# A sample's state update is issued behind the weight split written in front of it

## The chip, the core and the metric

The kernel runs on one core of a Trainium2 chip. The metric is the device time of one execution in microseconds; three runs of the kernel before took between 1820.84 and 1825.6 us, with a median of 1822.57 us. The engines are named as in the profile: PE (TensorE) multiplies matrices, DVE (VectorE) and ACT (ScalarE) work element by element, POOL (GpSimd) and SP (SyncE) here mostly issue DMA transfers. Each engine takes its own instructions strictly one after the other: an instruction that waits holds up everything behind it on the same engine.

## What is computed

One layer of a decoder runs for 256 positions of a prompt and for one new position of each of 8 samples, 264 columns in all. A wide projection feeds three branches: a spatial gate (A), an HGRN2 recurrence (B) and a gated linear attention, GLA (C). The branches are projected, gated, summed and projected again; then comes an MLP with 8192 hidden channels. For the samples the two recurrences are a single step on a stored state:

```
S_new = f[:, None] * S_old + k[:, None] * v[None, :]     # one head: 128 x 128 (HGRN2) or 128 x 256 (GLA)
o     = S_new.T @ q
```

There are 8 HGRN2 heads and 4 GLA heads for each of 8 samples. Each S_new is an output, and o goes on into the layer.

## The kernel before

**The weights.** All weights stream from memory through one long list of items, each a block of four 128-row slices by 256 columns (two slices by 512 columns at one place). SP loads an item into raw tiles (`raw`, line 623; four buffers). Products are made at full precision by splitting every weight in two: ACT casts one half of an item, 128x512, to `whi` (line 631), and DVE subtracts it from the raw value to give `wlo` (line 633, through the helper at line 113). There are six buffers each of `whi` and `wlo`, that is, three items of two halves. PE multiplies an item with three products for each tile (lines 671 to 673: `whi` by the high part of the activations, `whi` by their low part, `wlo` by the high part). One item so multiplied is a "granule" below: 24 products, 12 for each half.

At the end of a granule `ahead()` writes the split of the items up to three ahead of the one just multiplied. After granule number n, therefore, 2(n + 3) halves have been written. The split of the last of them needs the buffers that granule n has just given back.

**The work beside it.** After each granule `background()` (line 725) runs. It raises a counter `now` and takes steps from generators: `bg` with the prompt's recurrences (`mixer_r`) and `bs` with the samples' state updates (`samples_r`, line 1105). There are three groups, two of HGRN2 with four heads and one step per sample, and the GLA group with two steps per sample (two heads each): 32 steps in all.

A step n of `samples_r` writes, in this order: POOL's fetch of the state of step n+2 (`st`, line 1120; four buffers), POOL's broadcast load of the values of step n+1 from a scratch in memory (`vbc`, line 1126; two buffers), a pause until the state of step n was fetched three granules ago and its values two granules ago (`FETCHED`, line 1143), ACT's scaling of the state by f (line 1146, one instruction per head), DVE's multiply-add of k and v (line 1148, one per head), and POOL's store of the result (line 1149). When a sample is complete it is queued for `slot()` (line 692), where PE multiplies the state with q (line 712) at least two granules later; a fetch into a buffer waits for that product to have read it.

**Who orders what.** In this part of the kernel the written order is binding for PE and POOL alone (`manual_schedule`, line 1011). For DVE, ACT and SP the framework's scheduler chooses the order of the queue when the program is built, from its own estimates of when each instruction will be ready. Semaphores guard the data whichever order it chooses.

Of the kernel before, what the change touches and what calls it, by code (L numbers as in the profile page):

```python
# [7 lines left out]
F32 = mybir.dt.float32  # L8
F32R = mybir.dt.float32r
I32 = mybir.dt.int32  # L10
AF = mybir.ActivationFunctionType
ALU = mybir.AluOpType
# [6 lines left out]
NP = 256  # L19
# [45 lines left out]
def hybrid_step_kernel(  # L65
# [9 lines left out]
    V, S, T = nc.vector, nc.scalar, nc.tensor  # L75
# [13 lines left out]
    def nm(s):  # L89
        uid[0] += 1  # L90
        return f"{s}_{uid[0]}"

    def blk(shape=None, dt=F32):
        shape = shape or [P, 4, NT]
        return blkp.tile(shape, dt, tag="b", name=nm("b"))
# [4 lines left out]
    def tmp(shape, tag, bufs=2):  # L100
        return tp.tile(shape, F32, tag=tag, name=nm(tag), bufs=bufs)
# [4 lines left out]
    def mul(o, a, b):  # L106
        V.tensor_tensor(o, a, b, op=ALU.mult)  # L107
# [4 lines left out]
    def sub(o, a, b):  # L112
        V.tensor_tensor(o, a, b, op=ALU.subtract)  # L113
# [100 lines left out]
    def rstd_small(ms, scale, out):  # L214

        n, w = out.shape
        xx, aa = tmp([P, 16], "sx")[0:n, 0:w], tmp([P, 16], "sa")[0:n, 0:w]
        c = 0
        for m in ms if isinstance(ms, list) else [ms]:
            V.tensor_scalar(xx[:, c:c + m.shape[1]], m, scale, EPS, ALU.mult, ALU.add)  # L220
            c += m.shape[1]
        V.tensor_scalar(out.bitcast(I32), xx.bitcast(I32), -0.5, 1597463007.0, ALU.mult, ALU.add)
        for _ in range(3):
            mul(aa, out, out)
            V.scalar_tensor_tensor(aa, aa, -0.5, xx, ALU.mult, ALU.mult)
            V.scalar_tensor_tensor(out, aa, 1.5, out, ALU.add, ALU.mult)
# [370 lines left out]
    class Stream:  # L597
# [28 lines left out]
        def half_hi(self, i):  # L626
            n, width = self.items[i][2], self.items[i][4]
            hi = splp.tile([P, n // 2, width], F32R, tag="whi", name=nm("whi"))
            lo = splp.tile([P, n // 2, width], F32R, tag="wlo", name=nm("wlo"))
            raw = self.raw[i].pop(0)  # L630
            S.copy(hi, raw)  # L631
            self.parts.setdefault(i, []).append((hi, lo))
            return lambda: sub(lo, raw, hi.bitcast(F32))

        def split_half(self, i):
            self.half_hi(i)()
# [22 lines left out]
    stream = []  # L659
# [445 lines left out]
    def samples_r(G):  # L1105

        dv = G.dv
        nj, nh = dv // P, 512 // dv
        q, k, g = G.q, G.k, G.g
        fs = tmp([P, 4, NS], "fs")  # L1110
        S.activation(fs, g[:, :, NP:NT], AF.Exp)
        qm = blk([P, 4, NS, 32])
        mul(qm, q[:, :, NP:NT].unsqueeze(3).to_broadcast([P, 4, NS, 32]),
            delta.rearrange("p (b c) -> p b c", b=NS).unsqueeze(1).to_broadcast([P, 4, NS, 32]))
        steps = [(b, h) for b in range(NS) for h in range(0, 4, nh)]
        ahead, vals = [], []

        def fetch(b, h):
            st = tmp([P, nh, dv], "st", ST_BUFS)
            nc.gpsimd.dma_start(st, G.s_in(b, h, nh))  # L1120
            ahead.append((st, now[0]))

        def values(b, h):
            v = tmp([P, 4, P], "vbc", VB_BUFS)
            r0 = 4 * nj * b + h * nj
            nc.gpsimd.dma_start(v, vs_d[G.i, r0:r0 + 4, :].partition_broadcast(P))
            vals.append((v.rearrange("p (h j) v -> p h (j v)", h=nh), now[0]))

        for s in steps[0:2]:
            fetch(*s)  # L1130
            yield
        values(*steps[0])
        yield
        os_ = tmp([P, dv], f"os{G.i}", 1)
        sts = []
        for n, (b, h0) in enumerate(steps):
            if n + 2 < len(steps):

                yield lambda: len(sts) + sum(len(x[3]) for x in samples) <= ST_BUFS - 3
                fetch(*steps[n + 2])  # L1140
            if n + 1 < len(steps):
                values(*steps[n + 1])
            yield lambda: now[0] >= max(ahead[0][1] + FETCHED, vals[0][1] + FETCHED - 1)
            st, v = ahead.pop(0)[0], vals.pop(0)[0]
            for i in range(nh):
                S.activation(st[:, i, :], st[:, i, :], AF.Copy, scale=fs[:, h0 + i, b:b + 1])  # L1146
            for i in range(nh):
                V.scalar_tensor_tensor(st[:, i, :], v[:, i, :], k[:, h0 + i, NP + b:NP + b + 1], st[:, i, :], ALU.mult, ALU.add)  # L1148
            nc.gpsimd.dma_start(G.s_out(b, h0, nh), st)  # L1149
            sts.append(st)  # L1150
            if h0 + nh == 4:
                samples.append((now[0], (G, qm, os_), b, sts))
                sts = []
            yield
        yield lambda: not samples
        yield READY
        ss, rr = tmp([P, 1], "sss", 1), tmp([P, 1], "srr", 1)
        S.activation(tmp([P, dv], "vt"), os_, AF.Square, accum_out=ss)
        rstd_small(ss, 1.0 / dv, rr)
        S.activation(os_, os_, AF.Copy, scale=rr)  # L1160
        G.os = os_
        yield

    def mixer_r(G):
# [18 lines left out]
        q, k, g = G.q, G.k, G.g  # L1183

        bs.g.append(samples_r(G))


# [660 lines left out]
```

## Time and profile before

One execution was profiled. It is the source of every line shown in the prediction.

| | |
|---|---|
| median of 3 runs | 1822.57 us |
| the profiled execution's own time | 1821.44 us |
| its span, first to last instruction | 1819.4 us |
| mean granted TensorE clock | 0.998 |
| DVE busy | 1179.1 us (65%) |
| ACT busy | 997.2 us (55%) |
| state scaling on ACT, line 1146 | 96 instructions, 37.2 us, first at 369.4 us, last at 791.1 us |
| state update on DVE, line 1148 | 96 instructions, 34.2 us, first at 382.4 us, last at 797.5 us |

In the lines of the profile `out<-in` names the tile written and those read, `L1148` is a line of the kernel, and "x96" counts instructions. "idle before" is the time that an engine sat without work just before the instructions of a group, with what ended it. A row of the waits reads: engine and line that waited, what it waited for, then total us, times, longest us. In a timeline the columns are start, duration (both us), engine, line, operation, tiles, count, and in brackets the idle time before with its releaser. A row that merges "x2" gives the time from the first's start to the last's end.

### The profile page before, as it was taken

The page shows a single profiled execution, that of the slowest core. Times are in us where ns is not written, and L with a number is a line of the kernel's source. Part 1 is how long each engine was busy: PE and PEld are TensorE (multiplying, and loading weights), DVE is VectorE, ACT ScalarE, POOL GpSimd, SP SyncE. Part 2 cuts the span into 40 slices and gives each one's busy share as a digit, 9 for nine tenths or more (in the row PEclk, how much of TensorE's full clock was granted, in tenths as well). Part 3 has the DMA queues.
Part 4 walks back from the last instruction along what each step waited for, and adds up shares of the span by engine and source line. Part 5 has one row for each costly group of instructions (what it writes and reads, how often), then busy time and mean ns, then how long its engine had stood idle before and what let it go on. Part 6 is the DMA issues. An engine that isn't in the chain of part 4 may idle for free.

```text
span 1819.4 us, 42092 instructions
## 1 busy us (share of the span) xinstructions
PE 1780.7 (98%) x16970; PEld 1690.5 (93%) x16970; DVE 1179.1 (65%) x2077; ACT 997.2 (55%) x1824; POOL 138.3 (8%) x228
## 2 busy tenths in 40 slices
PE   7999999999999999999999999999999999999998
PEld 5889999989989988989999989999999999999998
DVE  5566668787576686566555667555666666666666
ACT  5344454666756756655445666454554545454544
POOL 4222000111111111210000000000000000000000
PEclk9999999999999999999999999999999999999999
DMA  9997587788788788897978954877666666666663
GB/s 325 379 347 282 196 293 247 218 260 295 230 285 262 228 261 302 274 326 241 305 252 267 330 166 153 251 255 222 196 195 193 196 196 195 198 196 194 195 193 118
DMA packets 330179, 442.05 MB, mean 243 GB/s; under 512 B 14946, under 2 KB 276944, under 8 KB 329984
## 3 DMA queue, kind: packets, MB, share of 16 engines
q1 hardware_dynamic: 311872, 380.52, 64.7%
q0 software_dynamic: 17184, 57.85, 8.9%
q8 instruction: 133, 2.18, 0.5%
q10 hardware_dynamic: 928, 0.99, 0.2%
q14 instruction: 62, 0.51, 0.1%
HBM read 427.60 MB, written 11.70 MB: 241 GB/s over the span
## 4 chain that ended last, share of the span: by engine, by line
PE 83%; issue 3%; DVE 3%; DMA 3%; ACT 1%; POOL 0%; ACTq 0%; DVEq 0%; SPq 0%; POOLq 0%
PE mm L671 25%; PE mm L673 25%; PE mm L672 25%; PE ada L383 3%; DMA vbc<-vs_d 2%; DVE wlo L113 1%; PE ada L315 1%; PE sm L893 1%; DMA raw<-in_w_in_dram 1%; DVE b L113 1%; PE sm L712 0%; ACT whi L631 0%; PE sm L705 0%; DMA araw<-in_w_ada_dram 0%; PE sm L1617 0%
## 5 line engine op out<-in xcount | busy, mean ns | idle before, releaser
L671 PE MATMUL mm<-b,whi 128*128 128x264 f32 x4600 | 1284.5, 279 | 7.5 <-ACT b L116 3.9
L673 PE MATMUL mm<-b,wlo 128*128 128x264 f32 x4600 | 1272.5, 277 | 6.4 <-DVE wlo L113 4.9
L672 PE MATMUL mm<-b,whi 128*128 128x264 f32 x4600 | 1271.3, 276 | 0.7 <-DVE b L113 0.7
L113 DVE TENSOR_TENSOR wlo<-raw,whi 128x512 fp32r<-128x512 f32 x1136 | 768.8, 689 | 430.4 <-ACT whi L631 427.0
L631 ACT CAST whi<-raw 128x512 fp32r<-128x512 f32 x1136 | 689.0, 616 | 628.9 <-DVE wlo L113 318.9
L671 PEld LDWEIGHTS mm<-b,whi 128*128 128x128 f32 x4600 | 870.8, 189 | 48.2 <-issue 24.8
L673 PEld LDWEIGHTS mm<-b,wlo 128*128 128x128 f32 x4600 | 870.8, 189 | 8.6 <-DVE wlo L113 7.0
L672 PEld LDWEIGHTS mm<-b,whi 128*128 128x128 f32 x4600 | 871.1, 189 | 1.3 <-DVE b L113 1.1
L110 DVE TENSOR_TENSOR b<-b,mm 128x528 f32<-128x528 f32 (+1 forms) x137 | 95.6, 699 | 73.4 <-PE mm L673 65.8
L1148 DVE SCALAR_TENSOR_TENSOR st<-vbc,b,st 128x128 f32<-128x128 f32 (+1 forms) x96 | 34.2, 391 | 54.8 <-DMA vbc<-vs_d 49.9
L1146 ACT ACTIVATE st<-st,fs 128x128 f32<-128x128 f32 (+1 forms) x96 | 37.2, 431 | 51.7 <-DMA st<-in_state_hgrn_dram 29.5
L1785 POOL TENSOR_TENSOR gs<-b,G 128x16 f32<-128x16 f32 x1 | 0.2, 222 | 714.1 <-DVE b L110 714.1
L502 POOL DMA_DIRECT2D b<-in_w_ada_dram x64 | 46.3, 726 | 38.4 <-PE ada L315 31.6
L383 PE MATMUL ada<-araw,cT 128*32 128x512 f32 x296 | 40.8, 601 | 0.4 <-DMA araw<-in_w_ada_dram 0.4
L315 PE MATMUL ada<-b,cT 128*32 128x256 f32 (+1 forms) x640 | 35.2, 358 | 2.1 <-DMA b<-in_w_ada_dram 1.9
L107 DVE TENSOR_TENSOR b<-b,b 128x512 f32<-128x512 f32 (+1 forms) x47 | 34.0, 743 | 1.3 <-ACT b L1260 1.1
L1149 POOL DMA_DIRECT2D out_dram<-st x32 | 23.5, 736 | 132.0 <-DVE st L1148 132.0
L315 PEld LDWEIGHTS ada<-b,cT 128*32 128x32 f32 x640 | 18.2, 114 | 14.2 <-DMA b<-in_w_ada_dram 5.6
L383 PE MATMUL ada<-b,cT 128*32 128x512 f32 x216 | 26.2, 593 | 0.0
L113 DVE TENSOR_TENSOR b<-gt,b 128x528 fp32r<-128x528 f32 x32 | 22.8, 712 | 3.2
L113 DVE TENSOR_TENSOR b<-b 128x1024 f32<-128x1024 f32 (+1 forms) x24 | 24.4, 1019 | 0.0
L1671 ACT ACTIVATE b<-vt 128x528 fp32r<-128x528 f32 x32 | 22.9, 714 | 1.0
(366 smaller groups left out, 902.4 us busy)
## 6 DMA issues: line engine op xcount, KB each, us to landing
raw<-in_w_in_dram SPq DMA_DIRECT2D x231, 512.0 KB, 5.0
raw<-in_w_mlp_up_dram SPq DMA_DIRECT2D x128, 512.0 KB, 3.9
raw<-in_w_mlp_down_dram SPq DMA_DIRECT2D x128, 512.0 KB, 3.6
araw<-in_w_ada_dram SPq DMA_DIRECT2D x74, 512.0 KB, 5.7
b<-in_w_ada_dram SPq DMA_DIRECT2D x54, 512.0 KB, 6.4
b<-in_w_ada_dram POOLq DMA_DIRECT2D x48, 512.0 KB, 10.4
raw<-in_w_branch_dram SPq DMA_DIRECT2D x48, 512.0 KB, 4.5
raw<-in_w_out_dram SPq DMA_DIRECT2D x32, 512.0 KB, 4.9
```

The lines of the kernel that those rows point to most:

```text
L107: V.tensor_tensor(o, a, b, op=ALU.mult)
L110: V.tensor_tensor(o, a, b, op=ALU.add)
L113: V.tensor_tensor(o, a, b, op=ALU.subtract)
L315: T.matmul(acc[32 * j:32 * j + 32, 0:n], cT[:, k, :], w[:, n * j:n * j + n], start=k == 0, stop=k == KT - 1)
L383: T.matmul(self.acc[32 * j:32 * j + 32, :], cT[:, k, :], ws[j // 2][:, j % 2 * 512:j % 2 * 512 + 512], start=k == 0, stop=k == KT - 1)
L502: queue.dma_start(w[:, i], w1[k * P:(k + 1) * P, :, self.k0 * P:(self.k0 + self.n) * P])
L631: S.copy(hi, raw)
L671: T.matmul(o, a, xh(k + j), start=first and j == 0, stop=False)
L672: T.matmul(o, a, xl(k + j), start=False, stop=False)
L673: T.matmul(o, b, xh(k + j), start=False, stop=last and j == n - 1)
L1146: S.activation(st[:, i, :], st[:, i, :], AF.Copy, scale=fs[:, h0 + i, b:b + 1])
L1148: V.scalar_tensor_tensor(st[:, i, :], v[:, i, :], k[:, h0 + i, NP + b:NP + b + 1], st[:, i, :], ALU.mult, ALU.add)
```

## The change

`half_hi` keeps the last cast and the last subtraction that have been written. `samples_r` wraps the scaling and the update of each step in `issue_after`, which adds an edge from each ACT instruction in the block to that last cast and from each DVE instruction in it to that last subtraction. The edge is one of issue order on the same engine: it adds no semaphore. Nothing else changes: the same instructions, tiles, buffers and transfers, and the written order of PE and POOL is what it was.

```diff
@@ half_hi
-            S.copy(hi, raw)
+            self.last = [S.copy(hi, raw).ins, None]
             self.parts.setdefault(i, []).append((hi, lo))
-            return lambda: sub(lo, raw, hi.bitcast(F32))
+
+            def low():
+                self.last[1] = V.tensor_tensor(lo, raw, hi.bitcast(F32), op=ALU.subtract).ins
+
+            return low
@@ samples_r
-            for i in range(nh):
-                S.activation(st[:, i, :], st[:, i, :], AF.Copy, scale=fs[:, h0 + i, b:b + 1])
-            for i in range(nh):
-                V.scalar_tensor_tensor(st[:, i, :], v[:, i, :], k[:, h0 + i, NP + b:NP + b + 1], st[:, i, :], ALU.mult, ALU.add)
+            with tc.issue_after(stream[0].last[0]), tc.issue_after(stream[0].last[1]):
+                for i in range(nh):
+                    S.activation(st[:, i, :], st[:, i, :], AF.Copy, scale=fs[:, h0 + i, b:b + 1])
+                for i in range(nh):
+                    V.scalar_tensor_tensor(st[:, i, :], v[:, i, :], k[:, h0 + i, NP + b:NP + b + 1], st[:, i, :], ALU.mult, ALU.add)
```

## The prediction, made before the changed kernel was seen

> **What bounds the kernel now.** I read the page first, for who is busy.
>
> ```profile
> PE 1780.7 (98%) x16970; PEld 1690.5 (93%) x16970; DVE 1179.1 (65%) x2077; ACT 997.2 (55%) x1824; POOL 138.3 (8%) x228
> ```
>
> PE is busy 98% of the span. A change of order on ACT and DVE can only give back time in which PE stands still, or runs slow, while the state updates are going on. So the second view is the list of PE's waits from 340 to 820 us, the stretch of the state updates.
>
> ```profile
> PE mm L673 <- DVE wlo L113: 4.9, 6, 2.0
> PE sm L705 <- issue: 3.0, 2, 2.3
> PE mm L671 <- ACT whi L631: 1.3, 1, 1.3
> PE mm L673 <- issue: 1.1, 1, 1.1
> PE mm L671 <- ACT gt L1379: 1.0, 1, 1.0
> ```
>
> That is 11.3 us in 11 gaps, and this is the whole stake. Six times PE waits for a subtraction, once for a cast, once for ACT's gate. Three gaps ("issue") have no cause that the profile shows. The third view is the same list for all engines: why are DVE and ACT late?
>
> ```profile
> POOL st L1120 <- PE sm L712: 143.7, 11, 31.3
> POOL out_dram L1149 <- DVE st L1148: 132.0, 17, 28.2
> ...
> DVE st L1148 <- DMA vbc<-vs_d: 49.9, 18, 7.6
> ...
> ACT st L1146 <- DMA st<-in_state_hgrn_dram: 29.5, 9, 8.8
> ACT st L1146 <- DMA st<-in_state_gla_dram: 14.8, 8, 3.0
> ```
>
> DVE stands for 49.9 us in 18 waits with a state update at the head of its queue whose values have not landed; ACT stands for 44.3 us with a scaling whose state has not landed. Subtractions and casts that could run are queued behind them. One such place in detail: first the counts up to 772.89 us, then the timelines of POOL, DVE and PE.
>
> ```profile
> L673 PE MATMUL mm<-b,wlo 128*128 128x264 f32 x1731 | 480.4, 278 | 3.4 <-DVE wlo L113 1.9 <-issue 1.1
> L113 DVE TENSOR_TENSOR wlo<-raw,whi 128x512 fp32r<-128x512 f32 x416 | 274.8, 686 | 83.1 <-ACT whi L631 79.9 <-PE mm L672 1.9 <-PE sm L712 0.7
> ...
> L113 DVE TENSOR_TENSOR wlo<-araw,whi 128x512 fp32r<-128x512 f32 x20 | 12.9, 684 | 0.0
> ```
> ```profile
> 765.56 0.57 POOL L1126 DMA_DIRECT2D vbc<-vs_d  x1
> ```
> ```profile
> 772.90 0.88 DVE L1148 SCALAR_TENSOR_TENSOR st<-vbc,b,st 128x256 f32<-128x256 f32 x2 [7.61 <-DMA vbc<-vs_d]
> 773.70 1.29 DVE L113 TENSOR_TENSOR wlo<-raw,whi 128x512 fp32r<-128x512 f32 x2
> ...
> 777.76 3.70 DVE L113 TENSOR_TENSOR wlo<-raw,whi 128x512 fp32r<-128x512 f32 x6
> ```
> ```profile
> 778.50 0.38 PE L673 MATMUL mm<-b,wlo 128*128 128x264 f32 x1 [1.01 <-DVE wlo L113]
> ```
> ```profile
> 781.17 0.64 PE L712 MATMUL sm<-st,b 128*32 128x256 f32 x8
> ```
>
> PE has run 1731 of these products, four for each half, so it is 432.75 halves into the weights. DVE has subtracted 416 + 20 = 436, only 3.25 halves more, and has stood 7.61 us for values that POOL asked for at 765.56. This update (sample 5, second pair of heads) is written after granule 218, as I count it by following the loops' counters; by then 2 x (218 + 3) = 442 halves are written. The scheduler has put it six halves ahead of its written place. For the 32 steps I count 3 to 23 halves.
>
> **The change part by part.** It removes and adds no instruction. It moves 96 scalings and 96 updates back behind the cast or subtraction written last. On their own engine the moved ones cost the same (37.2 and 34.2 us in all), so what changes is who waits behind them.
>
> *What the waits become.* In its written place the update above follows half 442, whose buffer comes free when PE has done 436. At 772.89 PE still has 3.25 halves to go. A half is 12 products; their pitch stands in PE's timeline at the first stall:
>
> ```profile
> 394.32 0.28 PE L672 MATMUL mm<-b,whi 128*128 128x264 f32 x1
> 394.44 0.28 PE L673 MATMUL mm<-b,wlo 128*128 128x264 f32 x1
> 396.04 0.38 PE L671 MATMUL mm<-b,whi 128*128 128x264 f32 x1 [1.32 <-ACT whi L631]
> 396.25 0.28 PE L672 MATMUL mm<-b,whi 128*128 128x264 f32 x1
> ```
>
> The pitch is 0.11 us, a half 1.3 us, a granule 2.7 us. So the update would come 3.25 x 1.3 = 4.3 us later at the earliest, when the values have long landed. In general, values are asked for at least two granules (5.4 us) ahead of the update's place and are followed by about 1.3 us of cast and subtraction: 6.7 us.
>
> ```profile
> DMA to landing us min/median/max: 3.7/6.6/9.3
> ```
>
> Half of the loads land inside that, the slowest are 2.6 us late. DVE then waits with all splits up to three items ahead done, 8.1 us of PE work. So I cost the remaining wait of DVE at nothing, covered by those items; without that cover it would cost up to 2.6 us a step. The states, fetched three granules (8.1 us) ahead, likewise.
>
> *What comes back on PE.* I assign to the state steps the waits for `wlo` except one (382.49, below), the wait for `whi` and the one for the gate: 4.9 - 0.6 + 1.3 + 1.0 = 6.6 us in seven gaps. A gap costs more than its idle time. From 394.44 to 396.04 are 1.60 us where 0.11 is usual, the next step takes 0.21, so 1.59 us are lost where 1.32 is shown: 0.27 more each, 7 x 0.27 = 1.9 us. And the clock:
>
> ```profile
> 380.00:400.00 20.00, 17.76 (x256) 16.14 (x256) 14.40 (x31) 9.15 (x19) 2.79 (x4) 0.94 0.76 244
> 400.00:420.00 20.00, 20.00 (x361) 18.65 (x361) 17.53 (x33) 13.86 (x26) 4.06 (x7) 0.97 0.91 306
> ...
> 760.00:780.00 20.00, 18.99 (x171) 17.02 (x170) 9.79 (x19) 11.04 (x23) 3.98 (x6) 1.00 0.93 327
> 780.00:800.00 20.00, 17.97 (x162) 16.64 (x161) 11.40 (x22) 9.43 (x20) 6.00 (x9) 1.00 0.98 353
> ```
>
> After the first stall the granted clock (third column from the right) is 0.94 and then 0.97: 20 x 0.06 + 20 x 0.03 = 1.8 us lost. Later stalls left it at 1.00. Together 6.6 + 1.9 + 1.8 = 10.3 us.
>
> [...]
>
> *What is given back.* At two gaps something else is late next:
>
> ```profile
> 797.08 0.88 DVE L1148 SCALAR_TENSOR_TENSOR st<-vbc,b,st 128x256 f32<-128x256 f32 x2 [3.25 <-issue]
> ```
> ```profile
> 798.17 1.14 ACT L631 CAST whi<-raw 128x512 fp32r<-128x512 f32 x2 [3.45 <-DMA raw<-in_w_in_dram]
> ```
> ```profile
> 798.62 0.38 PE L673 MATMUL mm<-b,wlo 128*128 128x264 f32 x1 [2.03 <-DVE wlo L113]
> ```
> ```profile
> 710.78 0.90 ACT L1146 ACTIVATE st<-st,fs 128x256 f32<-128x256 f32 x2
> ```
> ```profile
> 712.88 0.38 PE L671 MATMUL mm<-b,whi 128*128 128x264 f32 x1 [0.97 <-ACT gt L1379]
> ```
>
> Before 798.62 the next weights land only for the cast at 798.17. Without the update in front, PE would go on at about 796.6, work a half (1.3 us) and then wait about 1.0 us for that cast. At 712.88 the gate comes after two scalings of 0.90 us together; without them about 0.3 us of this gap, restart counted, is left. Given back: 1.3 us, which leaves 9.0.
>
> *The new wait.* PE's product with the new state (line 712) follows the last update by two or three granules. Before, the profile shows PE hardly waiting for it:
>
> ```profile
> L712 PE MATMUL sm<-st,b 128*32 128x128 f32 (+1 forms) x192 | 11.3, 316 | 0.1
> ```
>
> In the example the fourth of the six subtractions from 777.76 is half 442 and ends near 780.2; the update then ends near 781.1, and PE comes at 781.17. So the slack there is nothing, though with the stall of 7.61 us on DVE in front, which would be gone. Bounds over the 17 such products that I count: nothing, or one microsecond and a restart at each, 17 x 1.27 = 21.6 us. I take 2.0 us, three tight places at 0.4 + 0.27 each, nearer to the row with slack. That leaves 7.0. On POOL the stores (132.0 us of waiting) and the fetches behind them move with the updates; POOL also waits 143.7 us for PE's product, which stays where it is, so I cost them at nothing. SP's loads are released by the subtractions and come earlier.
>
> *Two doubtful gaps.*
>
> ```profile
> 382.49 0.38 PE L673 MATMUL mm<-b,wlo 128*128 128x264 f32 x1 [0.59 <-DVE wlo L113]
> ```
> ```profile
> 563.20 0.38 PE L673 MATMUL mm<-b,wlo 128*128 128x264 f32 x1 [1.15 <-issue]
> ```
>
> Both follow crowded stretches in which hoisted steps take part, the first without any wait for a load. Bounds are nothing and 0.86 + 1.42 us with restarts; I take half, 1.1 us. The two gaps before line 705 stay. The sum is 7.0 + 1.1 = 8.1 us: 1821.44 - 8.1 = 1813.3 us for the profiled execution, 1814.5 on the median of the runs, which is 1.1 us above it.
>
> **The rivals.** *Loads are next* (0.22). The share of the DMA engines (second column from the right) is 0.93 and 0.98 from 760 to 800 us. If there, and at 712.88, every wait saved comes back as a wait for weights, what remains is the first stall and the three gaps
>
> ```profile
> 396.86 0.38 PE L673 MATMUL mm<-b,wlo 128*128 128x264 f32 x1 [0.33 <-DVE wlo L113]
> ```
> ```profile
> 518.48 0.38 PE L673 MATMUL mm<-b,wlo 128*128 128x264 f32 x1 [0.54 <-DVE wlo L113]
> ```
> ```profile
> 523.97 0.38 PE L673 MATMUL mm<-b,wlo 128*128 128x264 f32 x1 [0.41 <-DVE wlo L113]
> ```
>
> 1.32 + 0.33 + 0.54 + 0.41 us with 4 restarts and the clock are 5.5 us; less the 2.0 of the new wait, 3.5 us are gained: 1819.1 us. Against it: loads are issued when subtractions free a buffer, so they move forward too. [...]
>
> *It does not do what it says* (0.10). The edge gives an order, not a time. If the scheduler puts other late work ahead of the subtractions instead, the gaps stay: 1822.6 us.
>
> *Slower: PE waits for the state* (0.16). Price and place are those of the new wait: 1.27 us at each of the 17 products, 21.6 us, less the gain without them, 9.0 + 1.1 us, is 11.5 us slower: 1834.1 us. It decides where the subtractions run later behind PE than in this profile; at 0.9 us a product, restart counted, it costs 15.3 us and so exceeds the gain by about 0.3%. Against it: DVE loses up to 49.9 us of standing.
>
> **How the numbers follow.** My forecast (0.52) is a gain of 8 us, 1814.5 us. A measurement tells about 0.3%, 5.5 us, from no change. Faster than that takes the forecast and a little of the first rival: 0.53. Within it, the rest of that and the second: 0.31. Slower: 0.16. The range goes from all 11.3 us with 11 restarts and the clock recovered (16.1 us, 1806.5) to 1824, which leaves out the last rival.
>
> **What would show it.** Right: line 1148's wait for `vbc` falls from 49.9 us to under 20; PE's waits for `wlo` in 340 to 820 us fall below 2 us; the clock of 380 to 420 us is 1.00; the updates begin 3 to 23 halves later in the order of DVE. Wrong: line 712 shows idle time before it of over 3 us, or line 631's wait for raw weights grows by more than 5 us after 700 us, or the gaps stay while the waits on `vbc` go.

## The result, and the profile after

Over six runs of each, the kernel before took 1821.86 us (median; 1818.89 to 1825.6) and the changed one 1807.14 us (1805.63 to 1807.35). The ratio is 0.992, with a 95% interval of 0.9909 to 0.9932: 14.7 us faster. The profiled execution took 1805.63 us against 1821.44 before, its span is 1803.9 us against 1819.4. The direction and the mechanism are those of the forecast. The gain is nearly twice the 8.1 us that it named.

Line numbers move a little: the cast is still line 631, the subtraction is now 635, the three products 675 to 677, the product of line 705 is 709, the product with the state 716, its fetch 1124, the values' load 1130, the scaling 1151, the update 1153, the store 1154.

The page's busy time of the changed kernel:

```profile
PE 1775.1 (98%) x16970; PEld 1687.9 (94%) x16970; DVE 1183.0 (66%) x2077; ACT 1001.4 (56%) x1824; POOL 138.7 (8%) x228
```

The counts of instructions are those of before. PE is 5.6 us less busy with the same 16970 products, and the span is 15.5 us shorter: the larger part of the gain is idle time. Part of the rest is that a product is recorded longer just after a gap (0.38 us for 0.28 in the rows of the prediction), and there are fewer gaps. PE's waits of the changed kernel from 340 to 820 us, every row:

```profile
PE sm L709 <- issue: 1.0, 2, 0.6
PE mm L677 <- DVE wlo L635: 0.6, 1, 0.6
PE mm L677 <- issue: 0.5, 1, 0.5
```

Where 11 gaps with 11.3 us stood, there are 4 with 2.1. Every wait that the prediction put down to the state steps is gone. The same view of the changed kernel for all engines:

```profile
POOL out_dram L1154 <- DVE st L1153: 223.7, 31, 38.3
...
POOL st L1124 <- PE sm L716: 53.8, 10, 10.2
...
ACT whi L631 <- DMA raw<-in_w_in_dram: 9.9, 7, 2.6
```

DVE's row for `vbc` is down to 1.4 us (49.9 before), and ACT has no row for `st` any more (44.3). The waiting has moved to POOL: its stores wait 223.7 us for the later updates (132.0 before), and the fetches behind them wait less for PE's product (53.8, was 143.7). POOL has that time. The two groups on the page of the changed kernel (idle time is the first number after the last bar):

```profile
L1151 ACT ACTIVATE st<-st,fs 128x128 f32<-128x128 f32 (+1 forms) x96 | 35.1, 430 | 0.0
L1153 DVE SCALAR_TENSOR_TENSOR st<-vbc,b,st 128x128 f32<-128x128 f32 (+1 forms) x96 | 32.4, 390 | 3.7 <-DMA vbc<-vs_d 1.4
```

The moved instructions cost on their own engine a little less than before (35.1 for 37.2 us, 32.4 for 34.2) and stand idle 0.0 and 3.7 us in front.

Where the gain lies, by windows that hold the same stage; the first is of the kernel before, the second of the changed one (length, then busy time and count of PE, PEld, DVE, ACT, POOL, then granted clock, share of the DMA engines, GB/s):

```profile
320.00:875.00 555.00, 542.94 (x5822) 505.63 (x5820) 388.88 (x740) 351.12 (x709) 70.84 (x107) 1.00 0.82 267
```
```profile
320.00:860.00 540.00, 537.64 (x5816) 502.65 (x5815) 391.40 (x737) 354.79 (x708) 71.12 (x107) 1.00 0.83 274
```

The second is 15.0 us shorter with 6 PE instructions fewer, which at the usual pitch of 0.11 us are 0.7 us. So 14.3 of the 15.8 us lie in this stage. The same product of PE, found by its place in PE's order, starts 1.4 us earlier in the changed kernel already at 320 us, ahead of the first state update, and 15.8 us earlier at 800 us and at 1000 us: nothing is gained behind the updates.

The example of the prediction, sample 5's second pair, in the changed kernel: the counts up to 763.54 us, then POOL, DVE and PE.

```profile
L677 PE MATMUL mm<-b,wlo 128*128 128x264 f32 x1740 | 481.3, 277 | 1.1 <-DVE wlo L635 0.6 <-issue 0.5
L635 DVE TENSOR_TENSOR wlo<-raw,whi 128x512 fp32r<-128x512 f32 x422 | 279.8, 687 | 112.9 <-ACT whi L631 110.9 <-PE sm L716 1.3 <-PE mm L677 0.3
...
L635 DVE TENSOR_TENSOR wlo<-araw,whi 128x512 fp32r<-128x512 f32 x20 | 12.9, 684 | 0.0
```
```profile
753.37 0.57 POOL L1130 DMA_DIRECT2D vbc<-vs_d  x1
```
```profile
763.55 0.88 DVE L1153 SCALAR_TENSOR_TENSOR st<-vbc,b,st 128x256 f32<-128x256 f32 x2
```
```profile
767.70 0.64 PE L716 MATMUL sm<-st,b 128*32 128x256 f32 x8
```

Exactly 422 + 20 = 442 halves have been subtracted, the number of the written place. The values were asked for 10.2 us earlier and the update starts with no idle time. It ends at 764.43, and PE multiplies the state at 767.70, 3.3 us later. All 32 steps stand so, with exactly the written number of halves ahead of them on ACT and on DVE.

### The profile page after: what moved, and what is told of

Same layout as the page of the kernel before. It is cut to its first block, busy times and chain, and to the rows that moved or that the text cites. A ratio compares the mean times of both kernels' runs of the same rounds, so it can differ in the third digit from the quotient of the medians.

```text
span 1803.9 us, 42121 instructions
## 1 busy us (share of the span) xinstructions
PE 1775.1 (98%) x16970; PEld 1687.9 (94%) x16970; DVE 1183.0 (66%) x2077; ACT 1001.4 (56%) x1824; POOL 138.7 (8%) x228
## 4 chain that ended last, share of the span: by engine, by line
PE 91%; DVE 1%; ACT 1%; issue 0%; DMA 0%; ACTq 0%; SPq 0%; DVEq 0%
PE mm L675 28%; PE mm L676 27%; PE mm L677 27%; PE ada L383 3%; PE ada L315 1%; PE sm L709 1%; PE sm L897 1%; PE sm L716 1%; DMA araw<-in_w_ada_dram 0%; DVE wlo L635 0%; PE sm L1622 0%; PE sm L1253 0%; DVE b L113 0%; DVE b L1602 0%; PE sm L1004 0%
## 5 line engine op out<-in xcount | busy, mean ns | idle before, releaser
L1154 POOL DMA_DIRECT2D out_dram<-st x32 | 23.6, 737 | 223.7 <-DVE st L1153 223.7
L1151 ACT ACTIVATE st<-st,fs 128x128 f32<-128x128 f32 (+1 forms) x96 | 35.1, 430 | 0.0
L1153 DVE SCALAR_TENSOR_TENSOR st<-vbc,b,st 128x128 f32<-128x128 f32 (+1 forms) x96 | 32.4, 390 | 3.7 <-DMA vbc<-vs_d 1.4
## 6 DMA issues: line engine op xcount, KB each, us to landing
b<-in_w_ada_dram POOLq DMA_DIRECT2D x48, 512.0 KB, 10.5
```

## The experiments

Eight kernels tell the theories apart. W is the theory of the prediction: a scaling or an update at the head of a queue waits for a load, and the casts and subtractions behind it come late. V puts it all on DVE's own queue. C says that the early place itself, the crowding of hoisted work in front of the splits, is the harm, load or no load.

### ACT's edge alone

Against the changed kernel:

```diff
-            with tc.issue_after(stream[0].last[0]), tc.issue_after(stream[0].last[1]):
+            with tc.issue_after(stream[0].last[0]):
```

> The edge on ACT alone; the updates on DVE are free again. Theory W (the gain is that no scaling or update waits for a load at the head of a queue with casts or subtractions behind it): an update needs its scaling, so the scheduler cannot put it far ahead; ACT's wait for states goes from 44.3 us to under 5, DVE's wait for values stays under 10, and the time is 1807 to 1810 us. Rival V (what counts is DVE's own queue): DVE still waits over 20 us for values, 1814 to 1819 us.

Measured: 1806.73 us (5 runs), ratio to before 0.9921 [0.9907, 0.9935]. That is the whole change. PE's waits in the stage are 1.0 + 0.6 + 0.6 us. The scaling in this kernel's page:

```profile
L1151 ACT ACTIVATE st<-st,fs 128x128 f32<-128x128 f32 (+1 forms) x96 | 35.0, 427 | 0.0
```

W is right (the time is even 0.3 us under its range). V's forecast fails, but V's cause isn't tested here, because with DVE left free DVE's waits went too, to 1.0 us. The update reads what its scaling wrote, and in this kernel the scheduler set all 32 updates at the very places that they have with both edges, with the same number of halves ahead of them. V falls further below, where the values alone are taken away.

### DVE's edge alone

```diff
-            with tc.issue_after(stream[0].last[0]), tc.issue_after(stream[0].last[1]):
+            with tc.issue_after(stream[0].last[1]):
```

> The edge on DVE alone; the scalings on ACT are free again. Theory W: ACT still stands some 30 to 45 us for states with casts behind it, and PE keeps one to three gaps: 1809 to 1815 us. Rival V (DVE's queue is all): as with both edges, 1806 to 1808 us.

Measured: 1838.14 us (4 runs), ratio 1.0091 [1.0074, 1.0109]: 17.5 us slower than before. No theory had that. The scaling's group in this kernel's page, then one place in the timelines of ACT, DVE, POOL and PE:

```profile
L1151 ACT ACTIVATE st<-st,fs 128x128 f32<-128x128 f32 (+1 forms) x96 | 37.2, 430 | 76.6 <-DMA st<-in_state_gla_dram 44.1
```
```profile
783.23 0.91 ACT L1151 ACTIVATE st<-st,fs 128x256 f32<-128x256 f32 x2 [5.96 <-issue]
784.05 2.69 ACT L631 CAST whi<-raw 128x512 fp32r<-128x512 f32 x5
```
```profile
784.68 1.29 DVE L635 TENSOR_TENSOR wlo<-raw,whi 128x512 fp32r<-128x512 f32 x2 [6.75 <-ACT whi L631]
785.90 0.87 DVE L1153 SCALAR_TENSOR_TENSOR st<-vbc,b,st 128x256 f32<-128x256 f32 x2
```
```profile
787.06 0.71 POOL L1154 DMA_DIRECT2D out_dram<-st  x1 [9.41 <-DVE st L1153]
787.77 0.72 POOL L1124 DMA_DIRECT2D st<-in_state_gla_dram  x1
```
```profile
794.25 0.51 ACT L1151 ACTIVATE st<-st,fs 128x256 f32<-128x256 f32 x1 [7.51 <-DMA st<-in_state_gla_dram]
```
```profile
796.44 1.03 PE L716 MATMUL sm<-st,b 128*32 128x256 f32 x2 [4.41 <-DVE st L1153]
```

Read from top to bottom it is a loop. ACT stands 5.96 us before a scaling (the profile names no releaser; counted in order, this scaling's state is the one whose fetch POOL issued at 776.36), so the casts come late; DVE stands 6.75 us for them; the update, bound behind its subtractions, comes after that; POOL's store waits 9.41 us for the update, and the next fetch is queued behind the store; the next scaling, still hoisted, waits 7.51 us for that fetch. ACT's waits for states rise from 44.3 to 70.5 us (44.1 + 26.4), and the product with the state, with 0.1 us of idle time in all before, waits 4.41 us here. Before, an early update let the store and the fetch go early. This kernel binds the end of the step and leaves its beginning hoisted. PE's two largest waits here, from 340 to 840 us:

```profile
PE sm L709 <- DVE b L107: 5.0, 1, 5.0
PE sm L716 <- DVE st L1153: 4.6, 2, 4.4
```

The first is for a step of the prompt, which stood in DVE's queue behind a subtraction; ACT had stood 5.31 us for a state there. All ten rows of PE add up to 23.0 us, for 11.3 before, and the clock fell twice in this stretch (last section).

### The loop cut: DVE's edge, and nothing to wait for

The kernel above, with the state and the values read from a constant tile. The fetch of the state goes into a tile that nobody reads, and the values' load, with one buffer, is read by nobody either.

```diff
+            got = tmp([P, nh, dv], "got", 1)
+            nc.gpsimd.dma_start(got, G.s_in(b, h, nh))
-            nc.gpsimd.dma_start(st, G.s_in(b, h, nh))
...
+            v = s0 = cst[:, 0:512].rearrange("p (h v) -> p h v", h=nh)
...
-                    S.activation(st[:, i, :], st[:, i, :], AF.Copy, scale=fs[:, h0 + i, b:b + 1])
+                    S.activation(st[:, i, :], s0[:, i, :], AF.Copy, scale=fs[:, h0 + i, b:b + 1])
```

> The edge on DVE alone, as in the run that was 17 us slower, but scaling and update read a constant tile and the transfers run unread (state outputs are not the reference's). Theory L (that run was slow because a scaling far ahead waits on ACT for a state whose fetch stands on POOL behind the store of an earlier update, and that update stands behind casts queued after the scaling): without the wait for the state the loop is cut, 1806 to 1811 us. Rival T (updates in written place are too late for PE's product when the scaling is not moved with them): 1825 to 1838 us.

Measured: 1809.73 us (6 runs), ratio 0.9934 [0.9922, 0.9947]. The same edge, 28.4 us faster than with the real state: the loop is what made it slow, not the late update in itself. The largest wait of PE left in the stage is one for a cast:

```profile
PE mm L675 <- ACT whi L631: 2.5, 1, 2.5
```

### The early place kept, the wait taken away

The kernel before, free order, with the constant tile as in the last experiment.

```diff
+            got = tmp([P, nh, dv], "got", 1)
+            nc.gpsimd.dma_start(got, G.s_in(b, h, nh))
-            nc.gpsimd.dma_start(st, G.s_in(b, h, nh))
...
+            v = s0 = cst[:, 0:512].rearrange("p (h v) -> p h v", h=nh)
-                S.activation(st[:, i, :], st[:, i, :], AF.Copy, scale=fs[:, h0 + i, b:b + 1])
+                S.activation(st[:, i, :], s0[:, i, :], AF.Copy, scale=fs[:, h0 + i, b:b + 1])
```

> No edge, but nobody waits for a state or its values: scaling and update read a constant tile, the transfers run as before into tiles that nobody reads (state outputs and what follows from them are so not the reference's). The scheduler may put the steps even further ahead than in the kernel before. Theory W: without waits on loads the early place costs little; PE's gaps of 340 to 820 us fall from 11.3 us to under 4: 1806 to 1811 us. Rival C (the early place itself is the harm: work that crowds ACT and DVE ahead of the splits): the gaps stay above 8 us, 1817 to 1823 us.

Measured: 1810.22 us (6 runs), ratio 0.9942 [0.9928, 0.9956]: 10.4 us faster than the kernel before in the same runs, with the hoisted order kept. PE's waits of this kernel in 340 to 820 us:

```profile
PE sm L705 <- issue: 2.8, 2, 2.5
PE mm L671 <- ACT att L1228: 1.4, 1, 1.4
PE mm L673 <- DVE wlo L113: 0.6, 1, 0.6
```

All `wlo` waits but the one of 0.6 us are gone, as are the one for the cast and the one for the gate. Counted as above, the steps stand as far ahead as in the kernel before, or further. W is right, and C falls as the cause of the 11.3 us: 4.8 us of gaps are left, a little more than the 4 that W allowed, and the time is inside W's range. What is left against the changed kernel is the gap before line 705 (2.8 us for 1.0), of which below, and the 1.4 us for `att`, a wait that neither the kernel before nor the changed one has. That this is a price of the early place is not shown.

### Only the values taken away

The kernel before, with `v` from the constant tile and the state's fetch as it was.

```diff
+            v = cst[:, 0:512].rearrange("p (h v) -> p h v", h=nh)
```

> No edge; only the update's values come from a constant tile (the broadcast loads still run unread; state outputs are not the reference's), while ACT still waits for the states. Theory W: DVE's 49.9 us of waiting for values become waits for ACT's scaling, shorter by what the state lands earlier; ACT's 44 us stay; a third to two thirds of the gain, 1811 to 1818 us. Rival V (DVE's wait for values is all): 1806 to 1810 us. Rival C: 1818 to 1823 us.

Measured: 1816.75 us (11 runs), ratio 0.9975 [0.9966, 0.9983]: 3.9 us faster than before in the same runs, so a part only. From this kernel's page:

```profile
L1147 ACT ACTIVATE st<-st,fs 128x128 f32<-128x128 f32 (+1 forms) x96 | 37.1, 430 | 54.8 <-DMA st<-in_state_hgrn_dram 29.3
L1149 DVE SCALAR_TENSOR_TENSOR st<-cst,b,st 128x128 f32<-128x128 f32 (+1 forms) x96 | 34.3, 393 | 33.5 <-ACT st L1147 33.1
```

ACT stands 54.8 us, 54.7 of it for states (51.7 before, of which 44.3 are listed under states), and DVE, which has no values to wait for, now stands 33.1 us for ACT's scaling. In the profile of before that wait was hidden behind the one for `vbc`, which came last. In the prediction's example, too, the scaling that the update needs had only just ended when DVE went on at 772.90. ACT had stood 7.32 us before it, which the profile puts down to PE:

```profile
771.95 0.91 ACT L1146 ACTIVATE st<-st,fs 128x256 f32<-128x256 f32 x2 [7.32 <-PE mm L673]
```

Both loads hold the queue, and taking one away uncovers the other. V falls here: it had 1806 to 1810 us. How the 3.9 us come about is less clear: PE's waits in 340 to 820 us are 10.5 us in all (11.3 before), with less for `wlo` (1.4 for 4.9) and more for the cast (2.5 for 1.3) and before line 705 (4.1 for 3.0), and in the profiled execution the clock did not fall in this stage, which is worth 1.7 us (last section).

### The same transfers taken out altogether

As in the experiment that keeps the early place, and the 64 transfers of states and values (16.8 MB) aren't issued.

```diff
-            nc.gpsimd.dma_start(st, G.s_in(b, h, nh))
...
-            nc.gpsimd.dma_start(v, vs_d[G.i, r0:r0 + 4, :].partition_broadcast(P))
```

> The order without edges and without waits for loads, and now without the 64 transfers of states and values too (16.8 MB less on the DMA engines; state outputs are not the reference's). It asks for the gaps of PE whose cause the profile does not show ('issue', 2.8 us before line 705 in the same kernel with the transfers). Theory I (PE waits there for its own instructions, whose load stands among the data transfers): these gaps fall below 1.5 us, 1805 to 1808 us. Rival: they do not depend on the transfers and stay at 2.5 us or more, 1809 to 1811 us.

Measured: 1805.26 us (4 runs), ratio 0.9912 [0.99, 0.9925]. PE's waits in 340 to 820 us:

```profile
PE mm L673 <- DVE wlo L113: 0.6, 1, 0.6
PE sm L705 <- issue: 0.5, 1, 0.5
PE sm L705 <- DVE b L107: 0.2, 1, 0.2
```

The gap before line 705 is 0.5 us, where with the same order and the transfers it was 2.8. That is theory I's size: with these transfers gone, in the same order, PE stands there for less. And with all these transfers gone the time is only about 2 us below the changed kernel's, with intervals that overlap. The changed kernel hides nearly all of them.

### Bound four halves earlier

```diff
-            self.last = [S.copy(hi, raw).ins, None]
+            self.past = (self.past + [[S.copy(hi, raw).ins, None]])[-5:]
+            last, self.last = self.past[-1], self.past[0]
...
-                self.last[1] = V.tensor_tensor(lo, raw, hi.bitcast(F32), op=ALU.subtract).ins
+                last[1] = V.tensor_tensor(lo, raw, hi.bitcast(F32), op=ALU.subtract).ins
```

> Both edges, but to the cast and the subtraction four halves (two granules) before the last written ones, so a step may come that much early. Theory W: values are asked for two granules ahead, so an update at that place meets its load just issued; DVE's wait for values comes back to 15 to 40 us and part of PE's gaps with it: 1809 to 1816 us. Rival F (what matters is only that steps cannot run ahead by ten or twenty halves): 1806 to 1808 us, as with the change.

Measured: 1808.09 us (6 runs), ratio 0.993 [0.9916, 0.9944]. One row of DVE's waits and all of PE's in 340 to 820 us:

```profile
DVE st L1155 <- DMA vbc<-vs_d: 16.1, 10, 3.1
```
```profile
PE sm L711 <- issue: 2.1, 2, 1.8
PE mm L679 <- DVE wlo L637: 0.6, 1, 0.6
```

W is half right. DVE waits for values again, 16.1 us in ten waits, as W had it, but none reaches PE. When the longest of them (3.06 us) began, DVE had subtracted 452 halves and PE had multiplied 446.5, and when it ended PE still had 3.25 halves to go; the one of 7.61 us in the prediction's example began 8 halves ahead and ended 3.25 ahead, and a second one of 1.98 us followed it. The time is what F said. So the exact place isn't what matters here. DVE stood 3.06 us with 5.5 halves split ahead (7.2 us of PE's work at 1.3 us a half) and PE did not wait; in the example it stood 7.61 + 1.98 = 9.59 us with 8 halves ahead (10.4 us), and PE waited 1.01 us.

### Every background step bound

The edges put on each step of the background generators, the prompt's recurrences among them.

```diff
-                c = next(self.g[0])
+                with tc.issue_after(stream[0].last[0]), tc.issue_after(stream[0].last[1]):
+                    c = next(self.g[0])
```

> The changed kernel, with the edges on every step of the background work (the prompt's recurrences too), not on the state steps alone. Theory W: the prompt's steps wait for no load, so there is nothing more to take away but the one gap before 382 us (0.6 us); on the other side PE may wait for prompt steps that come later: 1806 to 1812 us. Rival C (any work ahead of the splits is harm): 1803 to 1805 us.

Measured: 1822.79 us (12 runs, 1819.48 to 1827.38), ratio 1.0007 [0.9997, 1.0017]. The whole gain is lost, and both theories missed that. PE's first waits in 300 to 840 us:

```profile
PE sm L251 <- DVE vsb L110: 4.0, 2, 2.8
PE sm L1254 <- DVE b L107: 3.5, 3, 1.8
PE sm L1339 <- ACT b L1330: 1.2, 3, 0.4
```

The waits of the splits stay small; new are waits of PE for the prompt's own steps, on whose results PE's next products hang. For those steps the early place was of use. These rows name 8.7 us of the 13.8 by which this execution's span (1817.7 us) exceeds the changed kernel's. At the 0.27 us of a restart each, the eight gaps come to 2.2 us more (an estimate); the rest I can't put to rows.

## Why the prediction came out as it did

**The stake and its cause** held. The seven gaps assigned to the state steps (6.6 us) are gone, and the experiment that keeps the order and takes the loads away shows their cause: the load at the head of the queue. The update of 797.08, shown in the prediction, has the queue at work. DVE stands 3.25 us in front of it; the profile names no releaser. Counted in order, the four subtractions behind it belong to casts that ended from 792.62 to 794.21, the last of which is the first row here; they run only from 797.88, and PE waits 2.03 us for the first:

```profile
793.59 0.62 ACT L631 CAST whi<-raw 128x512 fp32r<-128x512 f32 x1
```
```profile
797.08 0.88 DVE L1148 SCALAR_TENSOR_TENSOR st<-vbc,b,st 128x256 f32<-128x256 f32 x2 [3.25 <-issue]
797.88 1.28 DVE L113 TENSOR_TENSOR wlo<-raw,whi 128x512 fp32r<-128x512 f32 x2
```

**The clock** term (1.8 us) held in this execution. The two windows of the changed kernel:

```profile
380.00:400.00 20.00, 19.41 (x285) 18.08 (x283) 18.00 (x35) 14.54 (x29) 2.05 (x4) 1.00 0.94 308
400.00:420.00 20.00, 20.00 (x422) 17.77 (x422) 16.97 (x35) 13.82 (x28) 6.01 (x9) 1.00 0.95 313
```

Both are at 1.00. In finer windows of the kernel before, the clock is 0.92, 0.50 and 0.73 from 396 to 402 us, two us each: 1.7 us, so the term is 0.1 too large. How sure such a price is, is another matter (last section).

**The step that failed first: "given back", 1.3 us.** It held the landing times of the weights fixed while moving the subtractions that release them, although the rival "loads are next" was answered with just that argument. The weights account for 1.0 of the 1.3 us; the other 0.3 were a rest of PE's wait for the gate. Measured, 0 for both: neither wait has a row in the changed kernel. ACT's waits for raw weights, before (700 to 820 us) and changed (684 to 804 us, with five us more of the work at the start, in which there is no such wait):

```profile
ACT whi L631 <- DMA raw<-in_w_in_dram: 7.9, 3, 3.4
```
```profile
ACT whi L631 <- DMA raw<-in_w_in_dram: 7.4, 4, 2.6
```

The longest is 0.8 us shorter, and none reaches PE. The loads moved forward with the subtractions. The DMA share of 0.98 and the 353 GB/s of the prediction's last window were no limit; one window of the changed kernel showed 1.03 and moved 379:

```profile
760.00:780.00 20.00, 20.00 (x182) 18.86 (x181) 13.12 (x23) 11.27 (x22) 5.48 (x10) 1.00 1.03 379
```

**The second: "the new wait", 2.0 us.** The slack of line 716 was read off in a place where DVE was 7.61 us late, and the change takes just that lateness away. The prediction said so itself and kept the term. Measured, 0: the slack in the example is 3.3 us, and over all 192 products of the changed kernel there is 0.1 us of idle time.

```profile
L716 PE MATMUL sm<-st,b 128*32 128x128 f32 (+1 forms) x192 | 11.6, 316 | 0.1
```

The rival that was to be slower had the same error in it. Its mechanism exists, as the kernel with DVE's edge alone shows (4.41 us at that product), but it takes a step whose beginning is left hoisted.

**The third: "the two gaps before line 705 stay".** They shrank from 3.0 to 1.0 us. The largest of before, then the same place in the changed kernel, found by the count of PE's products:

```profile
671.39 0.55 PE L705 MATMUL sm<-b 128*32 128x32 f32 x38 [2.29 <-issue]
```
```profile
660.44 0.57 PE L709 MATMUL sm<-b 128*32 128x32 f32 x42 [0.34 <-issue]
```

The other gap of before, 0.75 us at 541.51, is gone, and one of 0.65 us stands at 667.74, where before there was none. The profile names no instruction of ACT or DVE as the releaser of these products; the last section shows what such gaps go with. At this one place the gap is 2.29 to 2.62 us in the three kernels without edges that keep the transfers, 0.46 without the transfers, 0.31 to 0.34 in the changed kernel, with ACT's edge alone and with every step bound, 0.83 with DVE's edge and nothing to wait for, and 1.84 in the kernel bound four halves earlier; with DVE's edge alone there is none. So it depends on what else is moving, and goes with the order too; how the order does that is not shown.

**The two doubtful gaps** came out about as taken: the first is still there (0.6 us), the second is 0.5 instead of 1.15; 0.6 gained for the 1.1 forecast. The second is of the same kind as the gaps before line 705 (last section), so its shrinking isn't shown to come from the state steps.

**The sum.** 8.1 + 1.3 + 2.0 + 2.0 - 0.5 = 12.9 us, of 14.3 in this stage. Of the 1.4 us left, 0.5 is idle time too short for the list of waits (the windows show 12.06 - 2.36 = 9.7 us less, the lists 9.2); 0.9 stays open. So the mechanism was right, and the sum fell short by three terms that each assumed the old timing of something else.

## What to carry to other kernels

An instruction that a scheduler puts early on an engine cost little here as long as it waited for no load (4.8 us of gaps on PE in the early place without the loads, 11.3 with them); when it waits for one, it holds what is queued behind it, as at 797.08 in the kernel before, so bind the steps that wait for transfers, and leave the others hoisted. Bind such a step from its first instruction on: half a binding can close a loop through a store and the next fetch (17.5 us slower here, where the whole one is 14.7 faster). When a stall is taken away, work out the slack of what follows anew, loads included, since times read inside the stall carry it with them.

## What the runs showed of the hardware

**Gaps without a semaphore.** PE's "issue" gaps come just after packets of the queue that the profile calls `instruction`. The DMA view of the kernel before, 669.00 to 670.10 us, during the 2.29 us gap:

```profile
q0 software_dynamic: 84, 0.27, 66.5%
q1 hardware_dynamic: 58, 0.11, 27.8%
q8 instruction: 1, 0.02, 5.9%
```

One packet of the instruction queue (0.02 MB) ends at 670.07, and PE goes on at 671.39. The page counts 133 such packets on q8 for the 33,940 instructions of PE and PEld, one for some 255, so I take them for PE's instructions. All 22 "issue" gaps of PE of over 0.25 us between 340 and 840 us, in the ten kernels, end 1.2 to 1.6 us after such a packet. The packet's start differs: before, it comes at 669.03, after the start of PE's last product at 668.91; in the kernel without the transfers it comes at 657.78, with the last product at 659.44 and a gap of 0.46 us. So the gap of 2.29 us stands in a burst of 64 short products (26 before it, 38 behind), and its packet started 0.12 us after PE's last product; for the gap of 0.46 us it had started 1.66 us before.

**The clock after short gaps.** Before, the granted clock fell once in this stage, to 0.50 for 3.4 us (397.7 to 401.1), after the gap of 1.60 us (start to start) at 394.44, as the prediction's rows show; a gap of 0.61 us followed after two products. It fell after gaps of 4.79 and 5.26 us in the kernel with DVE's edge alone, and after one of 2.81 us in the kernel with that edge and nothing to wait for. It did not fall after 2.48 us (before, at 668.91), 2.69 (early place kept), 2.82 (values alone taken away), 3.03 (every step bound) and 3.25 (DVE's edge alone), nor after the 14 other gaps of 1.4 to 2.3 us in this stage of the ten kernels. As the clock fell after 2.81 us and not after 2.82 or 3.25, the length of the gap alone does not decide it. A short gap may cost clock, then, and the 1.8 us of the forecast were no fixed price. Over many runs the share may be larger: the mean granted clock is 0.9968 in 17 runs of the kernel before and 0.9986 in the five of the kernel with ACT's edge that were measured alongside. Over a span of 1806 us that difference is 3 us, an estimate.
